# Scan of a hybrid RWKV-7 step: the second stage of an adaLN block moves from the PSUM bank of U to that of Y

## The chip, the cores and the metric

The kernel runs on one core of one Trainium2 chip. The metric is the device time of one execution, in microseconds, as the median over repeated runs. Engines are named as in the profile: PE (matrix products), DVE and ACT (vector and scalar engine), POOL, and SP, whose queue issues most DMAs.

## What is computed

One inference step of a trunk of two layers with D = 1024: a bidirectional RWKV-7 mixer, then neighbourhood attention, each followed by an MLP. There are 128 context tokens and 512 latent tokens. Each sub-layer is modulated by shift, scale and gate from a conditioning vector ("adaLN"); each direction of RWKV-7 runs a delta-rule scan over the tokens:

```python
def ada_mod(cond, w, b):
    m = jax.nn.silu(cond) @ w + b
    return jnp.split(m, 6, axis=-1)
...
def delta_rule_scan(r, w, k, v, kk, a, s0, reverse):
    def step(S, inp):
        r_t, w_t, k_t, v_t, kk_t, a_t = inp
        sa = jnp.einsum('bhvk,bhk->bhv', S, -kk_t)
        S_new = (S * w_t[:, :, None, :] + sa[..., None] * (kk_t * a_t)[:, :, None, :]
                 + v_t[..., None] * k_t[:, :, None, :]).astype(S.dtype)
        y = jnp.einsum('bhvk,bhk->bhv', S_new, r_t)
        return S_new, y
...
    y = (ys[0] + ys[1]).astype(jnp.float32)
    mean = jnp.mean(y, axis=-1, keepdims=True)
    var = jnp.mean(jnp.square(y - mean), axis=-1, keepdims=True)
    yn = ((y - mean) * lax.rsqrt(var + GN_EPS)).reshape(B, T, D) * ln_w + ln_b
    o = (yn + (bonuses[0] + bonuses[1]).reshape(B, T, D)) * g
```

## The kernel before

The scan (`phase_scan`, line 773) works in chunks of 32 tokens. It has five steps n = 0 to 4 of four rounds e = 0 to 3, and in each round one chunk for each direction d = 0 and 1 (`chain_step`, line 1001). A chunk is a chain of four stages. R is the product of the state with the chunk's keys, copied to SBUF (`Rc`, L1035, on ACT). U is the product of Rc with TT, the inverse of a triangular matrix; four GU activations (L1052, ACT) write it into the buffer GU. The state update adds the chunk's products to bank B of its direction, and L1106 (DVE) or L1108 (ACT) copies it into the next GU; where a decay is due, L1111 (DVE) scales the bank. Y is the product of the state with the queries; a copy (L1069, ACT) or, where the other direction has been there already, an addition (L1067, DVE) reads it. R, U and Y of a direction use one PSUM bank A in turn (pool `ch`, one buffer), so each waits for the reader of the one before.

All matmuls of the scan, TensorE's order among them, are pinned by `mm` (line 850) in the order of the code. In a round that is: R d0; what is left of the round before (state update d1 and Y d1, where the fills allow it); U d0; fills; the first stage of an ada block; fills; R d1; state update d0; Y d0; U d1; fills; state update d1. The fills prepare the next step (`prep_group`, line 949): products into a tile `pp`, copies of them on ACT (invA L972, C L974) and a masked product on DVE (L977); POOL, DVE (the scans L916) and ACT (L917, L918, L939) prepare its elements. When a step's fills are done, `invert` (line 979) inverts the triangular matrices on DVE: a mask (L984), a transposition, thirty steps of L993 and L996, and a last transposition to TT (L998), without which the next step's U can't run.

The adaLN sums of layer 0 are made in blocks. `ada_first` (line 279) loads two weight tiles and sums over them on PE, and a copy to SBUF (L289, ACT) follows. `ada_second` (line 292) has two matmuls into four columns of a PSUM tile and one addition on DVE (L300, `mods`). Sixteen blocks of this kind lie in the scan, one first stage in a round; the second stage stands in the next chain step of direction 1 behind its U:

```python
        ut = self.ch.tile([P, 512], F32, name=f"A{d}")
        U = ut[:, :256]
...
        if self.ada_sums and d == 1:
            self.ada_second(*self.ada_sums.pop(0), ut[:, 256:260], self.mm)
        with tc.high_priority():
```

Finished pairs of chunks go through `post_half` (line 1114): loads of V (L1130), the gate (L1131) and factors (L1129) on SP's queue into a buffer `pbuf`; mean (L1136, L1137, L1139), square (L1140, ACT), variance (L1142, L1143) and a root (L258 to L264); V times its factor (L1146) and more (L1147 to L1151); a transposition on PE (L1156); the product with the gate on DVE (L1160); a store on SP's queue (L1162). In step n = 4 the elementwise part runs on DVE, before that on POOL. `wo_first` (line 1182) begins the output projection (L1189 loads, L1191, L1192).

Apart from the pinned order on PE, the order of instructions on each engine comes from a list scheduler with a time model; `tc.high_priority()` puts the operations of the chain ahead of others.

## Time and profile before

| | |
|---|---|
| median of three runs | 2232.8 us (2231.12 to 2234.78) |
| profiled execution | 2239.71 us |
| its span in the trace | 2237.9 us |
| mean granted PE clock | 0.944 |
| PE busy | 2011.6 us (90%) |
| DVE busy | 1169.5 us (52%) |
| ACT busy | 857.0 us (38%) |
| POOL busy | 455.1 us (20%) |
| L1052, GU activations | 160, 60.0 us busy; 64.0 us idle before them for L300 |

The profiled execution took 1.8 us more than its span and 6.9 us more than the median of the runs. The scan lies between some 340 and 780 us of the span; the inversions start (L984) at 440.5, 523.5, 608.6 and 681.8 us in the steps n = 0 to 3. Behind 834 us the MLP, the attention and the second MLP follow, mostly on PE. A row of a timeline merges neighbouring instructions of one kind; in it a matmul of the program counts twice.

### The profile page before, as it was taken

The numbers are of one execution on the slowest core, as the hardware profiler recorded it, in microseconds if no ns is written. First come the engines' busy times: TensorE is split into PE (matmuls) and PEld (weight loads), VectorE is DVE, ScalarE is ACT, GpSimd is POOL, SyncE is SP. The second block draws the span as 40 slices with busy tenths as digits, with TensorE's granted clock in tenths as the row PEclk, the third lists the DMA queues.
The fourth block names the chain that finished last, engine by engine and source line by source line (L and its number), as shares of the span: only waits on it lengthen the run. The fifth ranks groups of instructions, "written<-read, shape, count | busy, mean of one in ns | idle before, by whom it ended". The sixth has DMA issues, their size and how long they took to land.

```text
span 2237.9 us, 44938 instructions
## 1 busy us (share of the span) xinstructions
PE 2011.6 (90%) x18604; PEld 1827.3 (82%) x18604; DVE 1169.5 (52%) x2592; ACT 857.0 (38%) x1712; POOL 455.1 (20%) x553
## 2 busy tenths in 40 slices
PE   6999988757665569999999999999999999999999
PEld 3777777646554568999999998889677999999999
DVE  6656658387679755433333434433666633434342
ACT  4544553546553414313131323221576331313130
POOL 0001275656542411101010110000232110101010
PEclk8997999978787788999999999999899999999999
DMA  6455764545433464323232223343310232222221
GB/s 242 147 157 155 229 205 135 173 133 166 129 132 96 112 187 141 105 76 111 72 111 76 86 76 119 132 135 92 110 57 31 75 122 76 76 76 76 76 74 69
DMA packets 161037, 260.03 MB, mean 116 GB/s; under 512 B 46528, under 2 KB 102976, under 8 KB 160832
## 3 DMA queue, kind: packets, MB, share of 16 engines
q1 hardware_dynamic: 152224, 244.05, 35.2%
q10 hardware_dynamic: 8608, 13.11, 1.7%
q8 instruction: 146, 2.39, 0.4%
q14 instruction: 59, 0.48, 0.1%
HBM read 218.18 MB, written 37.35 MB: 114 GB/s over the span
## 4 chain that ended last, share of the span: by engine, by line
PE 74%; DVE 13%; DMA 5%; POOL 3%; issue 2%; ACT 2%; SPq 1%; DVEq 0%; ACTq 0%; POOLq 0%
PE psl L205 54%; PE psl L239 3%; DVE invX L996 2%; PE ps L1525 2%; DVE invT L993 2%; POOL C L947 2%; PE po L1562 2%; PE pp L852 2%; PE pt L1550 2%; DVE C L977 1%; PE pp L1219 1%; PE psl L1265 1%; PE psl L286 1%; DMA ld_s<-scr 1%; PE A L852 1%
## 5 line engine op out<-in xcount | busy, mean ns | idle before, releaser
L191 ACT CAST whi<-wraw 128x1024 fp32r<-128x1024 f32 x178 | 186.6, 1049 | 731.5 <-PE psl L205 701.9
L205 PE MATMUL psl<-xh,whi 128*128 128x320 f32 (+1 forms) x1696 | 414.6, 317 | 9.6 <-ACT xh L247 4.9
L205 PE MATMUL psl<-xl,whi 128*128 128x320 f32 (+1 forms) x1696 | 410.2, 314 | 1.2 <-DVE xl L248 1.2
L205 PE MATMUL psl<-xh,wlo 128*128 128x320 f32 (+1 forms) x1696 | 409.7, 314 | 0.4 <-DVE ta L592 0.4
L205 PEld LDWEIGHTS psl<-xh,whi 128*128 128x128 f32 x1696 | 291.4, 191 | 28.5 <-issue 8.7
L205 PEld LDWEIGHTS psl<-xl,whi 128*128 128x128 f32 x1696 | 292.5, 191 | 5.7 <-issue 3.2
L205 PEld LDWEIGHTS psl<-xh,wlo 128*128 128x128 f32 x1696 | 292.9, 191 | 2.6 <-issue 1.7
L1172 DVE SCALAR_TENSOR_TENSOR xres<-psl,mods,xres 128x320 f32<-128x320 f32 (+2 forms) x216 | 81.7, 434 | 305.1 <-PE psl L205 305.1
L1345 POOL TENSOR_TENSOR relu<-relu 128x640 f32<-128x640 f32 x64 | 80.2, 1255 | 773.9 <-ACT relu L1344 758.7
L205 PE MATMUL psl<-hhl,whi 128*128 128x320 f32 x1024 | 233.1, 308 | 0.0
L205 PE MATMUL psl<-hhh,wlo 128*128 128x320 f32 x1024 | 233.0, 308 | 0.0
L205 PE MATMUL psl<-hhh,whi 128*128 128x320 f32 x1024 | 232.9, 308 | 0.0
L193 DVE TENSOR_TENSOR wlo<-wraw,whi 128x1024 fp32r<-128x1024 f32 x178 | 218.6, 1229 | 11.6 <-ACT whi L191 10.9
L205 PEld LDWEIGHTS psl<-hhh,whi 128*128 128x128 f32 x1024 | 170.8, 188 | 0.4 <-issue 0.4
L205 PEld LDWEIGHTS psl<-hhh,wlo 128*128 128x128 f32 x1024 | 171.1, 188 | 0.0
L205 PEld LDWEIGHTS psl<-hhl,whi 128*128 128x128 f32 x1024 | 171.0, 188 | 0.0
L1302 DVE TENSOR_TENSOR relu<-psl,rms_b 128x320 f32<-128x320 f32 x128 | 60.8, 486 | 144.6 <-PE psl L205 144.0
L852 PE MATMUL pp<-C,KB 128*64 128x128 f32 x1280 | 100.6, 306 | 39.7 <-DVE C L977 16.7
L852 PEld LDWEIGHTS pp<-C,KB 128*64 128x64 f32 x1280 | 83.0, 154 | 54.1 <-issue 28.8
L248 DVE TENSOR_TENSOR hhl<-relu,hhh 128x640 fp32r<-128x640 f32 x64 | 53.4, 834 | 127.9 <-ACT hhh L247 127.7
L1052 ACT ACTIVATE GU<-A 32x256 f32<-32x256 f32 x160 | 60.0, 375 | 93.2 <-DVE mods L300 64.0
L977 DVE TENSOR_TENSOR C<-pp,cstsb 64x512 f32<-64x512 f32 x80 | 55.0, 688 | 69.1 <-ACT C L974 56.9
(299 smaller groups left out, 3393.2 us busy)
## 6 DMA issues: line engine op xcount, KB each, us to landing
wraw<-in_mlp_w SPq DMA_DIRECT2D x128, 512.0 KB, 3.5
adaraw<-in_ada_w SPq DMA_DIRECT2D x96, 512.0 KB, 4.9
ld_d<-scr SPq DMA_DIRECT2D x20, 512.0 KB, 4.5
ld_s<-scr SPq DMA_DIRECT2D x20, 512.0 KB, 3.7
bias<-in_bias SPq DMA_DIRECT2D x16, 384.0 KB, 3.7
scr<-ta SPq DMA_DIRECT2D x16, 325.0 KB, 3.5
wi<-scr SPq DMA_DIRECT2D x20, 260.0 KB, 4.6
scr<-bp SPq DMA_DIRECT2D x16, 320.0 KB, 4.5
```

What stands on the lines that cost most here:

```text
L191: nc.scalar.copy(hi, raw)
L193: nc.vector.tensor_tensor(lo, raw, hi.bitcast(F32), op=ALU.subtract)
L205: self.nc.tensor.matmul(ps[g][:, :e - c], lhsT=a[:, k, :], rhs=b[:, c:e], start=(k == 0 and j == 0), stop=(k == n - 1 and j == 2))
L239: nc.tensor.matmul(ps, lhsT=a[:, tc_], rhs=w, start=(k == 0 and j == 0), stop=(k == KT - 1 and j == 2))
L248: (lo_eng or nc.vector).tensor_tensor(xl, src, xh.bitcast(F32), op=ALU.subtract)
L852: r = (op or self.nc.tensor.matmul)(*a, **k)
L947: nc.gpsimd.tensor_tensor(rev(o) if s == 0 else o, v4(sh, s, ww)[hs], f[hs], op=ALU.mult)
L977: nc.vector.tensor_tensor(C[o, 8 * h:8 * h + 8, :], pn[o, :, 0:64], mask[o], op=ALU.mult)
L1052: nc.scalar.activation(gu[64 - 64 * hp:96 - 64 * hp, hp, pp].rearrange("p b v -> p (b v)"), U[32 * q:32 * q + 32, :], AF.Copy, scale=-0.5)
L1172: nc.vector.scalar_tensor_tensor(out[:, a:b], ps[g][:, o:o + b - a], gate[:, k, j:j + 1], x[:, a:b], op0=ALU.mult, op1=ALU.add)
L1302: nc.vector.tensor_tensor(t[:, c], ps[q][:, :HALF], rb[:, c], op=ALU.mult)
L1345: nc.gpsimd.tensor_tensor(t, t, t, op=ALU.mult)
```

## The change

`ada_second` leaves the second stage of the chain. Its columns 256 to 259 now lie in the bank of Y, and it stands behind Y's reader and inside `high_priority`, so that its matmuls and its addition have the priority of the chain. Nothing is computed otherwise.

```diff
--- before.py
+++ after.py
@@ -1021,30 +1021,28 @@
         C = [ts["C"][d, hg, ww] for hg in range(2)]
 
         def state_product(s):
-            ps = self.ch.tile([P, 512], F32, name=f"A{d}")[:, :256]
+            pa = self.ch.tile([P, 512], F32, name=f"A{d}")
+            ps = pa[:, :256]
             for ph, pp, hp in idx:
                 q = 2 * hp + pp
                 i = 8 * hp + 4 * ee + 2 * (ph % 2) + pp
                 self.mm(ps[32 * q:32 * q + 32, 64 * ph:64 * ph + 64], lhsT=C[ph // 2][:, i, 32 * s:32 * s + 32],
                         rhs=gu[:, hp, pp, ph, :], start=True, stop=True, tile_position=(0, 32 * q))
-            return ps
-
-        R = state_product(0)
+            return pa, ps
+
+        _, R = state_product(0)
         with tc.high_priority():
             Rc = self.yp.tile([P, 256], F32, name="Rc", bufs=2)
             nc.scalar.copy(Rc, R)
         yield
         TT = ts["TT"]
-        ut = self.ch.tile([P, 512], F32, name=f"A{d}")
-        U = ut[:, :256]
+        U = self.ch.tile([P, 512], F32, name=f"A{d}")[:, :256]
         for ph, pp, hp in idx:
             q = 2 * hp + pp
             o = slice(64 * ph, 64 * ph + 64)
             qs = slice(32 * q, 32 * q + 32)
             self.mm(U[qs, o], lhsT=TT[qs, d * 16 + ((ph // 2) * 4 + cq) * 2 + ph % 2, :],
                     rhs=Rc[qs, o], start=True, stop=True, tile_position=(32 * q, 32 * q))
-        if self.ada_sums and d == 1:
-            self.ada_second(*self.ada_sums.pop(0), ut[:, 256:260], self.mm)
         with tc.high_priority():
             for pp in range(2):
                 for hp in range(2):
@@ -1056,7 +1054,7 @@
             self.state_update(ts, n, e, d, gu, nx, C)
         self.gi[d] += 1
         yield
-        Y = state_product(1)
+        pa, Y = state_product(1)
         tt = ts["tiles"][d]
         with tc.high_priority():
             if tt not in self.yt:
@@ -1068,6 +1066,8 @@
             else:
                 nc.scalar.copy(yo, Y)
                 self.ydone[tt].add(cq)
+            if self.ada_sums and d == 1:
+                self.ada_second(*self.ada_sums.pop(0), pa[:, 256:260], self.mm)
         if e % 2 == 1:
             self.free[ts["par"]] += [ts["C"].pop((d, hg, ww)) for hg in range(2)]
         yield
```

In the changed kernel the lines between are numbered otherwise: Rc is L1036, GU L1050, Y's addition L1065 and its copy L1067.

The orders below show three places. The first is PE at the turn from round e = 0 to e = 1 of step n = 0: A_4169 or A_4166 is R d0, A_4188 or A_4185 is Y d1, A_4206 is U d0, `pp` are fills. Before:

```order
L852 MATMUL A_4169<-GU_3894,C_2648 32x64 [waits DMAHW2_49,PE_49]
L852 MATMUL A_4169<-GU_3894,C_2648 32x64
L852 MATMUL A_4169<-GU_3894,C_2648 32x64 [waits DMAHW3_49]
L852 MATMUL A_4169<-GU_3894,C_2648 32x64 x5
L852 MATMUL A_4169<-GU_3894,C_2656 32x64 x8
L852 MATMUL A_4188<-GU_2638,C_2652 32x64 [waits DVE_49]
L852 MATMUL A_4188<-GU_2638,C_2652 32x64 x7
L852 MATMUL A_4188<-GU_2638,C_2660 32x64 x8
L852 MATMUL A_4206<-Rc,TT 32x64 [waits Activation_49]
L852 MATMUL A_4206<-Rc,TT 32x64 x15
L852 MATMUL pp_4227<-C_3890,KB 64x128 [waits Pool_49] x2
L852 MATMUL pp_4227<-C_3890,KB 64x128 x6
```

And in the change, where the pair (`cstsb,adasb`) stands between Y d1 and U d0 and waits for ACT:

```order
L852 MATMUL A_4166<-GU_3894,C_2648 32x64 [waits DMAHW3_49]
L852 MATMUL A_4166<-GU_3894,C_2648 32x64 x5
L852 MATMUL A_4166<-GU_3894,C_2656 32x64 x8
L852 MATMUL A_4185<-GU_2638,C_2652 32x64 [waits PE_49]
L852 MATMUL A_4185<-GU_2638,C_2652 32x64 x7
L852 MATMUL A_4185<-GU_2638,C_2660 32x64 x8
L852 MATMUL A_4185<-cstsb,adasb 128x2 [waits Activation_49]
L852 MATMUL A_4185<-cstsb,adasb 128x2
L852 MATMUL A_4206<-Rc,TT 32x64 [waits PE_49]
L852 MATMUL A_4206<-Rc,TT 32x64 x15
L852 MATMUL pp_4227<-C_3890,KB 64x128 [waits Pool_49] x2
```

The pair came from behind U d1 of the round before; now U d0 and all fills are behind it and behind its wait.

The second place is DVE at the end of n = 3's inversion, with TT (L998). Before, L1160 runs ahead of TT, and behind it L1106 and Y's addition of direction 1 are followed by L1142, L1136, L1143 and L1192:

```order
L993 TENSOR_TENSOR invT_7843<-invX 128x10
L1160 TENSOR_TENSOR pbuf<-pp_8546,pbuf 128x256 x2
L996 TENSOR_TENSOR invX<-invX,invT_7843 128x10
L998 STREAM_TRANSPOSE TT<-invX 128x32x32
L1106 TENSOR_TENSOR GU_3897<-B_3880,FC 64x512 x2
L1111 TENSOR_TENSOR B_3880<-B_3880,FC 128x512
L1067 TENSOR_TENSOR Y<-Y,A_8421 128x256
L1142 TENSOR_REDUCE yvar<-pbuf 128x8
L1136 TENSOR_REDUCE ysum<-Y 128x8
L1143 TENSOR_SCALAR yvar<-yvar 128x8
L1192 TENSOR_TENSOR ww_9303<-adaraw,ww_9302 128x1024
L1137 TENSOR_SCALAR ysum<-ysum 128x8
```

In the change, L1106, L1111 and Y's addition of direction 0, L1136 to L1139 and L1160 stand behind TT:

```order
L996 TENSOR_TENSOR invX<-invX,invT_7840 128x10
L998 STREAM_TRANSPOSE TT<-invX 128x32x32
L1106 TENSOR_TENSOR GU_3894<-B_3879,FC 64x512 x2
L1111 TENSOR_TENSOR B_3879<-B_3879,FC 128x512
L1065 TENSOR_TENSOR Y<-Y,A_8293 128x256
L1136 TENSOR_REDUCE ysum<-Y 128x8
L1137 TENSOR_SCALAR ysum<-ysum 128x8
L1139 TENSOR_TENSOR Y<-Y,ysum 128x512
```

and these rows follow, in which an L1146 stands ahead of L1136, L1143, L1192 and the addition L300 of the last pair:

```order
L1160 TENSOR_TENSOR pbuf<-pp_8546,pbuf 128x256 x2
L1106 TENSOR_TENSOR GU_3897<-B_3880,FC 64x512 x2
L1111 TENSOR_TENSOR B_3880<-B_3880,FC 128x512
L1065 TENSOR_TENSOR Y<-Y,A_8418 128x256
L1142 TENSOR_REDUCE yvar<-pbuf 128x8
L1146 TENSOR_TENSOR pbuf<-pbuf,bc 128x512
L1136 TENSOR_REDUCE ysum<-Y 128x8
L1143 TENSOR_SCALAR yvar<-yvar 128x8
L1192 TENSOR_TENSOR ww_9303<-adaraw,ww_9302 128x1024
L300 TENSOR_TENSOR mods_96<-A_8418,parsb 128x4
```

Before, the two L1146 came nine and fourteen rows behind that L1142. So operations moved from ahead of TT to behind it, and one that waits for a load moved ahead.

The third place is SP's queue there. pbuf_8343 (in the change pbuf_8340) is stored by L1162, and pbuf_8565 uses the same buffer after it. Before, the loads of two `pbuf` tiles are mixed:

```order
L1162 DMA scr9<-pbuf_8343 128x8x64 [waits DMAHW4_49,DVE_49,Activation_49]
L1130 DMA pbuf_8565<-scr7 32x2x256 [waits DMAHW5_49,DMAHW4_49,Pool_49]
L1130 DMA pbuf_8565<-scr7 32x2x256 [waits DMAHW6_49]
L1130 DMA pbuf_8554<-scr7 32x2x256 [waits DMAHW0_49]
L1130 DMA pbuf_8554<-scr7 32x2x256 [waits DMAHW2_49]
L1130 DMA pbuf_8554<-scr7 32x2x256
L1130 DMA pbuf_8554<-scr7 32x2x256 [waits DMAHW6_49]
L1131 DMA pbuf_8554<-scr10 128x8x64 [waits DMAHW7_49]
L1130 DMA pbuf_8565<-scr7 32x2x256 [waits DMAHW0_49]
L1130 DMA pbuf_8565<-scr7 32x2x256 [waits DMAHW1_49]
L1131 DMA pbuf_8565<-scr10 128x8x64 [waits DMAHW2_49]
```

In the change the four loads of pbuf_8565, the first of which waits for the store, come first:

```order
L1162 DMA scr9<-pbuf_8340 128x8x64 [waits DMAHW4_49,DVE_49,Activation_49]
L1130 DMA pbuf_8565<-scr7 32x2x256 [waits DMAHW5_49,DMAHW4_49,Pool_49]
L1130 DMA pbuf_8565<-scr7 32x2x256 [waits DMAHW6_49]
L1130 DMA pbuf_8565<-scr7 32x2x256 [waits DMAHW7_49]
L1130 DMA pbuf_8565<-scr7 32x2x256 [waits DMAHW0_49]
L1131 DMA pbuf_8565<-scr10 128x8x64 [waits DMAHW1_49]
L1130 DMA pbuf_8554<-scr7 32x2x256 [waits DMAHW3_49]
L1130 DMA pbuf_8554<-scr7 32x2x256 [waits DMAHW5_49]
L1130 DMA pbuf_8554<-scr7 32x2x256 [waits DMAHW7_49]
L1130 DMA pbuf_8554<-scr7 32x2x256 [waits DMAHW1_49]
L1131 DMA pbuf_8554<-scr10 128x8x64 [waits DMAHW2_49]
```

On DVE the first L1146 of the change works on pbuf_8565; before it worked on pbuf_8554.

## Rows read from the trace of the kernel before

**Rows 1.** Chain of waits: engine, line, what it waits for: us, times, longest us

```profile
ACT GU L1052 <- DVE mods L300: 64.0, 15, 13.2
```

**Rows 2.** Busy time by stretches: length, PE (x) PEld DVE ACT POOL, PEclk, DMA share, GB/s

```profile
681.80:725.80 44.00, 22.88 (x560) 18.10 (x560) 43.42 (x152) 14.46 (x33) 11.09 (x9) 0.73 0.31 89
...
834.00:2237.00 1403.00, 1379.79 (x9753) 1305.06 (x9752) 597.83 (x1338) 464.42 (x849) 151.80 (x174) 0.99 0.29 91
```

**Rows 3.** Timeline, PE, n=1: start, us, engine, line, operation [idle before <-releaser]

```profile
504.92 0.61 PE L852 MATMUL A<-cstsb,adasb 128*128 128x2 f32 x4
```

**Rows 4.** Timeline, round n=0 e=1 and the start of n=0's inversion: PE, ACT, DVE

```profile
420.20 0.65 PE L852 MATMUL A<-Rc,TT 32*32 32x64 f32 x32 [0.64 <-ACT Rc L1035]
...
428.49 0.35 ACT L1069 COPY Y<-A 128x256 f32<-128x256 f32 x1
...
434.61 1.97 PE L852 MATMUL pp<-C,KB 128*64 128x128 f32 x32
...
438.87 1.06 ACT L972 COPY invA<-pp 32x128 f32<-32x128 f32 x4
...
439.09 1.39 DVE L1106 TENSOR_TENSOR GU<-B,FC 64x512 f32<-64x512 f32 x2 [2.37 <-PE B L852]
...
440.51 1.22 DVE L984 TENSOR_TENSOR invA<-invA,cstsb 128x1024 f32<-128x1024 f32 x1
```

**Rows 5.** Timeline, DVE, near the end of n=0's inversion

```profile
490.98 1.23 DVE L916 TENSOR_TENSOR_SCAN wi<-cstsb,wi 128x520 f32<-128x520 f32 x1
```

**Rows 6.** Timeline, n=1: ACT, PE, and DVE's start of the inversion

```profile
511.04 0.38 ACT L1069 COPY Y<-A 128x256 f32<-128x256 f32 x1
...
511.19 0.65 PE L852 MATMUL A<-Rc,TT 32*32 32x64 f32 x32 [0.65 <-ACT Rc L1035]
...
519.57 1.75 PE L852 MATMUL pp<-C,KB 128*64 128x128 f32 x28 [0.95 <-issue]
...
523.52 1.23 DVE L984 TENSOR_TENSOR invA<-invA,cstsb 128x1024 f32<-128x1024 f32 x1 [0.82 <-ACT invA L972]
```

**Rows 7.** Timeline, n=2: the last fill on PE, and DVE's start of the inversion

```profile
602.75 1.97 PE L852 MATMUL pp<-C,KB 128*64 128x128 f32 x32 [0.29 <-DVE C L977]
...
608.64 1.22 DVE L984 TENSOR_TENSOR invA<-invA,cstsb 128x1024 f32<-128x1024 f32 x1
```

**Rows 8.** Timeline, n=3: PE and ACT at the start, the last fill, DVE's inversion

```profile
652.88 0.65 PE L852 MATMUL A<-Rc,TT 32*32 32x64 f32 x32
...
653.25 0.35 ACT L1069 COPY Y<-A 128x256 f32<-128x256 f32 x1
...
675.79 1.97 PE L852 MATMUL pp<-C,KB 128*64 128x128 f32 x32
...
681.84 1.23 DVE L984 TENSOR_TENSOR invA<-invA,cstsb 128x1024 f32<-128x1024 f32 x1
```

**Rows 9.** Timeline, DVE, around the end of n=3's inversion (L998) and behind it

```profile
722.94 0.76 DVE L1160 TENSOR_TENSOR pbuf<-pp,pbuf 128x256 f32<-128x256 f32 x2
...
723.81 1.97 DVE L998 STREAM_TRANSPOSE TT<-invX 128x1024 f32<-128x1024 f32 x1
...
728.09 0.68 DVE L1142 TENSOR_REDUCE yvar<-pbuf 128x8 f32<-128x512 f32 x1
...
729.34 1.22 DVE L1192 TENSOR_TENSOR ww<-adaraw,ww 128x1024 fp32r<-128x1024 f32 x1
...
735.04 0.69 DVE L1146 TENSOR_TENSOR pbuf<-pbuf,bc 128x512 f32<-128x512 f32 x1 [0.52 <-issue]
```

**Rows 10.** Timeline, SP's queue; and the chain that ended last, a DMA in it

```profile
726.56 3.69 SPq L1130 DMA_DIRECT2D pbuf<-scr  x6
...
726.92 3.00 DMA pbuf<-scr
```

**Rows 11.** Timeline, PE: R d1 of n=4 e=0 and R d0 of the next round

```profile
728.22 1.08 PE L852 MATMUL A<-GU,C 128*32 128x64 f32 x32 [1.22 <-DVE Y L1067]
...
736.16 1.19 PE L852 MATMUL A<-GU,C 128*32 128x64 f32 x32 [3.10 <-ACT GU L1052]
```

## The prediction

> **What bounds the kernel now.** I read the chain of waits first, then the busy time by stretches, then the timeline step by step. The chain of waits shows the cost that the edit touches: the GU activations (L1052) wait 15 times and 64.0 us in all for the ada addition L300, 13.2 us at the longest [rows 1]. They read columns 0 to 255 of the bank, L300 reads 256 to 259: two readers of one bank run one after the other. The stretches show that little of the 64 us can be got. While a triangular inversion runs, DVE is the bound: 43.42 of 44.00 us busy in the last one; from 834 us to the end PE is busy 1379.79 of 1403.00 us, and nothing of that is touched [rows 2]. So a wait counts only between the end of one inversion (TT, L998) and the start of the next (L984): there the last GU stands on ACT ahead of the invA copies (L972), and L984 needs these.
>
> **What the change does.** It adds and removes no work: 16 pairs of matmuls at 0.6 us [rows 3] and 16 additions move. A pair stood on PE behind U d1 and was waited for by GU alone. It now stands behind Y d1 and waits for Y's reader, and U d0 of the next round, its fills and R d1 queue behind it. GU waits for PE alone. DVE's order shifts too, since the scheduler is run again. I go step by step to TT of n=4, then from there to the end, against the profiled execution (2239.71 us, 6.9 above the median of 2232.8).
>
> **n=0.** U d0 ran at 420.20; the copy of Y d1, late on ACT, ended at 428.49+0.35 = 428.84 [rows 4]. In the change U d0 starts behind it and the pair, at 429.4. R d1, which the same copy released, must now let 4 to 6 us of U and fills pass. Some of this is won back, as R's copy stood behind others on ACT; I put the last fill (434.61+1.97 = 436.58 before) at 440.8, invA's copies 1.06 behind it at 441.9, and L984 right there for 440.51 [rows 4]: +1.4, of which I take +1.3. The ends: if nothing is made up, L984 moves with the fill, +4.2; if the stall cost PE nothing, the fill would end 0.6 earlier (the pair is gone from behind U d1) at 436.0, and L984 could start at 437.0: -3.5. In the inversion behind it, the two L1106 (1.39) that stood ahead of L984 [rows 4] move in: +1.4. A scan L916 (1.23) [rows 5], a reduction L1142 and two small ones (0.8) move out behind TT: -2.05. Together **+0.65**.
>
> **n=1.** Y's copy ends at 511.42, with the pair 512.0; U d0 ran at 511.19: +0.8. The pair is gone from behind U d1: -0.6. The last fill thus ends at 521.32+0.2 = 521.5, GU and L917 no longer hold invA's copies, these end at 522.6, and L984 starts there for 523.52 [rows 6]: **-0.9**.
>
> **n=2.** By the same sum the fill ends at 604.72+0.2 = 604.9, L984 starts at 606.0 for 608.64 [rows 7]: -2.6; there it had stood behind two L1106, which now run behind it: +1.4. Together **-1.2**.
>
> **n=3.** Two pairs stand ahead of a U d0 here. The first costs 653.25+0.35+0.6-652.88 = 1.3 [rows 8]; the second, behind a Y addition on DVE, I put at 0.9, between this and n=1's. Two pairs gone from behind U d1: -1.2. The fill ends at 677.76+1.0 = 678.8, L984 starts at 680.0 for 681.84 [rows 8]: **-1.8**.
>
> **Last inversion.** Two L1106 (1.4), L1160 (0.76), three of the length of L1142 (0.68: L1111, L1136, L1139), a Y addition, L1137 and L300 move from inside to behind TT; an L1142 and small ones move in. By rows 4 and 9 that is some 4.5 out and 0.9 in: **-3.6**. TT of n=4 then ends at 0.65-0.9-1.2-1.8-3.6 = -6.9 against before, at 718.9 for 725.78 [rows 9].
>
> **Behind TT.** This gives the time back. Before, L1160 ran at 722.94, ahead of TT [rows 9]. SP's store L1162 waited for it, and the loads of V behind the store's landing began at 726.56: six issues in 3.69 us, 0.6 apart; the first landed at 726.92+3.00 = 729.92, 3.4 behind its issue [rows 10]. The fourth of four in a row would land at 726.56+1.8+3.4 = 731.8, that is 8.8 us behind the start of L1160. In the change L1160 stands behind TT and L1106, L1111, Y, L1136, L1137 and L1139: by L1106 to the start of L1142 (2.3 us behind TT's end before) and three more at 0.68, 0.17 and 0.68, some 3.9 us behind TT. SP now loads first the buffer that has to wait for the store, and DVE's first L1146 works on just this buffer; it stands ahead of L1136, L1143, two L1192 and L300, where before it stood behind them, at 735.04 with 0.5 us of waiting [rows 9]. So DVE can pass L1146 at 3.9+8.8 = 12.7 us behind TT. Before, it had what now stands behind L1146 still to do at the end of L1142, 728.77, or 3.0 behind TT. What follows is late by 12.7-3.0-0.5 = 9.2 less the 6.9 won: **+2.3 on DVE**. For PE: L1146 at 731.6, then L1136 (0.7), one L1192 (1.22) and a small one, and L300 at some 734.3 [rows 9]; R d1 writes into the bank that L300 reads and runs at 734.4 for 728.22. From there to R d0 of the next round PE needs 736.16-728.22-3.10 = 4.8 [rows 11]: 739.2 for 736.16, **+3.0**. The two meet before 747; I take +2.5, since the chain there runs through DVE, and carry it to the end: 2242.2 for the profiled execution, 6.9 less in the median: **2235.3 us**.
>
> **A rule weighed.** The trace shows two readers of one bank in turn [rows 1]; no row shows a matmul that waits for a reader of other columns. Without such a wait n=0 would be -3.5+1.4-2.05 = -4.2 for +0.65, and the 0.8, 0.8 and 2.2 that the pairs cost in n=1 to n=3 would go: 8.6 less, 2226.7. The order of the change shows the wait on the pair, so I give this no chance of its own. The Trainium skill, PSUM — Partial Sum Buffer, section "PSUM bank collisions raise a hardware error", says that any two engines on one bank and the same quarter of the partitions collide, TensorE's writes against a reader included and in disjoint columns too, and that one has to guard by bank. By that rule Y's bank is no freer than U's: the wait changes its owner, from ACT's GU to PE's queue, and the sum is mine. No run here shows a collision.
>
> **Rivals.** *Faster: the loads are not late.* If V has landed when DVE comes to L1146 (SP free sooner, the store and the landing quicker), nothing is given back and the end moves with TT, -6.9: 2225.9. For it: the 8.8 us rest on one store and one landing, in a stretch where other loads ran beside them. Against: the loads wait for the store by their buffer, and the store for L1160, which now runs behind TT. Decides: idle time of DVE ahead of that L1146 under 3 us. Chance 0.2.
> *Slower: TT gains little.* PE stands behind Y's reader, and the stall of n=0 is not made up. Then L984 of n=0 comes 4.2 late for 1.3, n=3 gives nothing for -1.8, and TT gains 6.9-2.9-1.8 = 2.2 us; with the 9.2 behind TT the end moves by +7.0: 2239.8. For it: in n=0 U d0 ran 8.6 us ahead of the end of Y's copy [rows 4], and n=3's first pair alone stands 1.3 us [rows 8]. Against: L984 waits for ACT, which is freed of GU's wait and L917. Decides: TT of n=4 ends later than 721.5. Chance 0.35.
> *Nothing.* The waits move from GU to U d0 and weigh as much; all else cancels: 2232.8. It lies in my own range, with chance 0.1; my forecast has 0.35.
>
> **How the numbers follow.** About 0.2%, 4.5 us, is what can be told from no change. My forecast (+2.5) and "nothing" lie within it: 0.45. Slower by more: the rival, 0.35. Faster by more: 0.2. The range reaches from the fast rival's time, 2226, to 2242, the slow one's with 2 us more for the store and the landing, which I have from one transfer each; half of the fast rival and the slow one's tail lie outside.
>
> **What would show it.** L1052's wait for L300 is gone from the chain of waits, and PE waits in front of the pair for ACT's L1067 (Y's copy) or DVE's L1065. Against before, L984 of n=0 comes 1 us later, those of n=2 and n=3 some 3 earlier; TT of n=4 ends near 719. Behind it DVE idles about 4 us ahead of L1146, and R d1, at 728.22 before, starts near 734. I am wrong if TT of n=4 ends outside 716 to 722, if DVE does not wait at that L1146, or if the last 1403 us change their length.

## The result and the profile after

The change takes 2251.6 us (median of five runs, 2247.5 to 2253.9) for 2232.9 in the kernel before: ratio 1.0079, with 1.0064 to 1.0094 as its 95% interval. (The ratios here are worked out from the single runs and are not the quotient of the two medians.) It is slower by 18.7 us, and lies 9.6 above the range that was forecast. In a second set of runs it is 2252.0 for 2238.7, ratio 1.0067 (1.0042 to 1.0092). In that and the later sets the kernel before had medians of 2236.2 to 2238.7 over 14 to 30 runs, so that some 3 to 6 us of the 18.7 may be owed to its five runs in the first. One run of a version below, after_first, took 2648.65 us at a granted clock of 0.69 and is in none of its figures. The profiled execution of the change took 2247.51 us, its span 2245.7.

The page of the change: its engines' work and the GU activations, which waited for L300 in [rows 1]. The last line is that of the GU activations on the page of the kernel before:

```profile
PE 2006.0 (89%) x18604; PEld 1823.9 (81%) x18604; DVE 1171.2 (52%) x2592; ACT 858.8 (38%) x1712; POOL 457.1 (20%) x553
...
L1050 ACT ACTIVATE GU<-A 32x256 f32<-32x256 f32 x160 | 60.0, 375 | 64.2 <-PE A L852 55.3
...
L1052 ACT ACTIVATE GU<-A 32x256 f32<-32x256 f32 x160 | 60.0, 375 | 93.2 <-DVE mods L300 64.0
```

The work is the same: as many matmuls, within 6 us of busy time on every engine. The wait for L300 is gone; ACT's idle time in front of GU fell from 93.2 to 64.2 us, most of it now a wait for PE. PE waits for Y's readers instead, in PE's waits over the whole span:

```profile
PE A L852 <- DVE Y L1065: 29.0, 9, 5.6
...
PE A L852 <- ACT Y L1067: 23.4, 10, 10.0
```

All 23.4 us of the second line are waits in front of a pair. Of the first line, 9.2 us in three waits are in front of an R, by PE's timeline; the 16 pairs have 23.4+19.9 = 43.3 us. They replace other waits in part: U's wait for Rc, 14.8 us in 14 times before, is 0.5 in one. The longest is in n=0, in the timeline of PE (start, length, operation, idle time and what ended it), where U d0 ran at 420.20 [rows 4]:

```profile
426.86 1.01 PE L852 MATMUL A<-cstsb,adasb 128*128 128x2 f32 x4 [9.97 <-ACT Y L1067]
427.80 1.07 PE L852 MATMUL A<-Rc,TT 32*32 32x64 f32 x32
```

Behind TT of n=4, DVE (its rows of before are [rows 9]):

```profile
716.31 1.91 DVE L998 STREAM_TRANSPOSE TT<-invX 128x1024 f32<-128x1024 f32 x1
718.08 1.36 DVE L1106 TENSOR_TENSOR GU<-B,FC 64x512 f32<-64x512 f32 x2
...
720.20 0.42 DVE L1065 TENSOR_TENSOR Y<-Y,A 128x256 f32<-128x256 f32 x1
...
722.26 0.75 DVE L1160 TENSOR_TENSOR pbuf<-pp,pbuf 128x256 f32<-128x256 f32 x2
...
726.27 0.68 DVE L1142 TENSOR_REDUCE yvar<-pbuf 128x8 f32<-128x512 f32 x1
730.60 0.69 DVE L1146 TENSOR_TENSOR pbuf<-pbuf,bc 128x512 f32<-128x512 f32 x1 [3.65 <-DMA wr<-in_xT]
...
733.01 0.15 DVE L300 TENSOR_TENSOR mods<-A,parsb 128x4 f32<-128x4 f32 x1
```

The store and loads of SP's queue, for [rows 10], and then PE, for [rows 11]. The store landed 2.6 us behind its issue, at 725.7, right ahead of the loads. The slowest of the four loads landed 3.5 us behind its issue at 727.0, at 730.5 and right ahead of L1146 at 730.60. I take it that L1146 waits for this load, though its row names another transfer:

```profile
723.07 0.38 SPq L1162 DMA_DIRECT2D scr<-pbuf  x1
725.71 1.73 SPq L1130 DMA_DIRECT2D pbuf<-scr  x4
```

```profile
720.67 1.08 PE L852 MATMUL A<-GU,C 128*32 128x64 f32 x32 [5.05 <-DVE Y L1065]
721.68 1.97 PE L852 MATMUL B<-GU,C 64*64 64x64 f32 x32
723.59 0.66 PE L852 MATMUL A<-GU,C 128*32 128x64 f32 x32
726.40 0.61 PE L852 MATMUL A<-cstsb,adasb 128*128 128x2 f32 x4 [2.16 <-DVE Y L1065]
726.94 1.01 PE L852 MATMUL A<-Rc,TT 32*32 32x64 f32 x32
733.22 1.08 PE L852 MATMUL A<-GU,C 128*32 128x64 f32 x32 [5.27 <-DVE mods L300]
...
739.20 0.77 PE L852 MATMUL A<-GU,C 128*32 128x64 f32 x32 [1.35 <-ACT GU L1050]
```

These are R d0, the state update, Y d1, the pair, U d0 (the first with the new TT), R d1 and R d0 of the next round. DVE waits at L1146, L300 runs behind it, R d1 behind L300. In the kernel before, R d0 and U d0 were:

```profile
718.80 1.08 PE L852 MATMUL A<-GU,C 128*32 128x64 f32 x32 [8.46 <-DVE Y L1067]
...
725.92 1.07 PE L852 MATMUL A<-Rc,TT 32*32 32x64 f32 x32 [1.34 <-DVE TT L998]
```

So before, R d0, state update and Y d1 ran ahead of TT (723.81), and U d0 2.1 us behind TT's start. Now they run behind TT, and U d0 is 10.6 us behind its start. The last stretch, from the scan's end to the end (us, then busy time of PE, PEld, DVE, ACT, POOL, and the granted clock), follows. The window of [rows 2] ends 0.9 us ahead of its span's end (2237.9), so that the stretch was 1403.9 us and has grown by 3.1:

```profile
838.70:2245.70 1407.00, 1380.97 (x9752) 1305.46 (x9752) 598.92 (x1338) 464.87 (x849) 151.91 (x174) 0.99 0.28 90
```

Three profiles of each kernel by stretches, in us, from starts read to 0.1 us ("input" is the first transfer of x behind the scan, L1237 in the kernel before, for what is left of the output projection; the expectations call it the attention's input. "Attention" is from the first to the last addition of its scores):

| stretch | before | change | means' difference | forecast |
|---|---|---|---|---|
| start to first TT | 393.1, 395.3, 391.0 | 390.5, 391.1, 390.7 | -2.4 | 0 |
| first to last TT | 330.7, 324.9, 326.1 | 325.8, 327.5, 330.4 | +0.6 | -6.9 |
| last TT to input | 110.2, 112.3, 110.0 | 122.4, 121.3, 123.5 | +11.6 | some +9.4 |
| input to attention | 744.2, 744.7, 744.2 | 744.4, 743.9, 743.7 | -0.4 | 0 |
| attention | 127.2, 126.8, 126.9 | 130.0, 130.0, 129.9 | +3.0 | 0 |
| behind it | 532.5, 532.6, 532.5 | 532.6, 532.4, 532.5 | 0 | 0 |

The sum is +12.4 (spans 2235.1 and 2247.5). Up to the first TT the profiles of both kernels show the same order on DVE, ACT and POOL, and no pair lies there. I take -2.4 as scatter between executions: over the profiles of all kernels on this page the first TT comes at 385.0 to 396.3 us. Two kernels below repeat these scans with only the attention reordered: att_new, the scan of before, has 334.6 us from first to last TT and 110.1 from there to the input; att_old, the scan of the change, 326.0 and 125.2. With them the means' difference is -1.7 from first to last TT and some +12 behind it. So by neither reckoning does the change gain some 7 us ahead of the last TT, and the loss behind it is clear of the scatter. Nor is that loss the granted clock (theory C below): from the last TT to the input it is 0.82, 0.78 and 0.82 in the three profiles of before and 0.79, 0.79 and 0.82 in those of the change, of which the one at 0.82 is the longest.

### The profile page after: what moved, and what is told of

The parts are those of the page before. It is cut to its first block, busy times and chain, and to the rows that moved or that the text cites. A ratio compares the mean times of both kernels' runs of the same rounds, so it can differ in the third digit from the quotient of the medians.

```text
span 2245.7 us, 44954 instructions
## 1 busy us (share of the span) xinstructions
PE 2006.0 (89%) x18604; PEld 1823.9 (81%) x18604; DVE 1171.2 (52%) x2592; ACT 858.8 (38%) x1712; POOL 457.1 (20%) x553
## 4 chain that ended last, share of the span: by engine, by line
PE 74%; DVE 14%; DMA 4%; issue 2%; POOL 2%; ACT 2%; SPq 1%; DVEq 0%; ACTq 0%; POOLq 0%
PE psl L205 53%; PE psl L239 4%; DVE invX L996 3%; DVE invT L993 3%; PE ps L1525 2%; PE pp L852 2%; PE po L1562 2%; POOL C L947 2%; PE pt L1550 2%; DVE C L977 1%; PE pp L1219 1%; PE psl L1265 1%; PE psl L286 1%; PE A L852 1%; PE pk L698 1%
## 5 line engine op out<-in xcount | busy, mean ns | idle before, releaser
L205 PE MATMUL psl<-xh,whi 128*128 128x320 f32 (+1 forms) x1696 | 412.4, 316 | 11.7 <-ACT xh L247 6.2
L1050 ACT ACTIVATE GU<-A 32x256 f32<-32x256 f32 x160 | 60.0, 375 | 64.2 <-PE A L852 55.3
```

What stands on the lines that cost most here:

```text
L205: self.nc.tensor.matmul(ps[g][:, :e - c], lhsT=a[:, k, :], rhs=b[:, c:e], start=(k == 0 and j == 0), stop=(k == n - 1 and j == 2))
L1050: nc.scalar.activation(gu[64 - 64 * hp:96 - 64 * hp, hp, pp].rearrange("p b v -> p (b v)"), U[32 * q:32 * q + 32, :], AF.Copy, scale=-0.5)
```

## Experiments

The theories are those of the expectations: W, orders and waits on DVE behind TT; S, PE's stand in front of the pair; C, the granted clock.

**The change and a pin on L1146**, beside each other. First the unchanged change:

> The changed kernel once more, with every execution's granted clock beside those of the kernel before. Two theories for its 18.7 us. W (waits and orders): DVE waits 3.65 us at an L1146 behind TT of n=4 and the pairs stand on PE; the profiled execution shows about 7 us of this between the first inversion and 834 us, so 7 to 10 us remain for the median, and the other 9 to 12 lie in how the one profiled execution of each kernel stood to its median. C (clock): a part of the loss is a lower granted clock, in which case executions of this kernel fall apart by clock (0.944 at 2247.5, 0.935 to 0.939 at 2249 to 2254 so far) and the kernel before shows a higher clock than the 0.944 of its profiled execution in its faster executions. Expected: 2249 to 2253 again; W: clock of both kernels alike, C: before at 0.947 or more.

2251.95 us, ratio 1.0067 (1.0042 to 1.0092): the loss is there again. The granted clock over an execution is 0.937 to 0.941 for 0.941 to 0.949 in the kernel before; where in the kernel it differs is read below. Then the pin:

```diff
+        vb = el.tensor_tensor(Vg, Vg, bcast(bc.rearrange("p c l -> p (c l)")), op=ALU.mult)
+        if on_dve and tt in (1, 2): self.tc.add_manual_dep(vb.ins, self.root.ins.name, order, reason="order")
```

> The changed kernel with one order on DVE undone: in the two halves that DVE treats in n=4, L1146 (V times its factor) may only run behind the root of its half, as the code has it; it no longer stands ahead of L1136, L1192 and L300. W: DVE's 3.65 us at L1146 go, L300 and R d1 come some 4 us earlier, and with what followed (the lower clock, 3.3 us more to the scan's end) the kernel gains 4 to 7 us: about 2245. S (the stands of PE behind Y's reader are what costs): 0 to 1 us gained, 2251. C: nothing, 2251.

2251.79 us, ratio 1.0063 (1.0040 to 1.0085), runs from 2239 to 2263. The wait at L1146 is gone and the last TT to input takes 117.7 us, in a second profile 119.2, for 121.3 to 125.2: some 3 to 5 us of the 11.6 hang on this wait. The median, which W had at 2245 and S and C at 2251, does not move; half of the runs are at 2255 or above, for a reason that the second profile shows (*More profiles*).

**Another bank for the pair**: the second bank of the fills' tile `pp`, one round later; then with the pin too.

```diff
+                    if self.ada_sums: self.ada_second(*self.ada_sums.pop(0), pa[:, 512:516], self.mm)
```

> The pair in neither bank of the chain: it writes into the second bank of the tile of the next block's first stage, just ahead of that stage's matmuls. GU then never waits for L300 and U never for Y's reader; the order with L1146 early behind TT stays as in the changed kernel. W: the wait at L1146 stays and swallows what is gained, so about 2244 to 2249. S: all stands of PE go (9.97 us in n=0 the longest), the kernel comes to 2233 or below. C: near 2250.

> Both: the pair in neither bank of the chain, and L1146 of the two halves behind the root. W: DVE does not wait behind TT, GU not for L300, PE not for Y's reader; below the kernel before, 2224 to 2231. S: as the kernel with the bank alone, since the order on DVE weighs nothing, about 2233 or below. C: near 2250, as its stretches with little PE work are the same.

2263.39 us (1.0092 to 1.0141) and 2252.59 (1.0044 to 1.0094); W and S had 2224 to 2249 and missed both; C, with near 2250, met the second. PE's waits in the first:

```profile
PE pp L852 <- DVE mods L300: 38.2, 15, 9.4
```

The wait has gone over to the fills; first to last TT grew to 339.5 us, in the second to 341.3.

**The pair in Y's bank, but behind U d0 and the first fills of the next round**, then with the pin:

```diff
-                self.ada_second(*self.ada_sums.pop(0), pa[:, 256:260], self.mm)
+                self.pair.append((*self.ada_sums.pop(0), pa[:, 256:260], self.mm))
```

> The pair keeps Y's bank, but stands on PE behind U d0 and the first fills of the next round instead of ahead of U d0, so that U d0 does not wait for Y's reader (10 us in n=0). L1146 still stands early behind TT. S: the scan gets shorter by what PE loses at Y's reader, to 443 or less, and the kernel is some 5 us faster than the changed one. W: the wait at L1146 stays, and what is won ahead of TT is lost behind it: 446 to 448, no gain over 2 us.

> The pair behind U d0 and the first fills, and L1146 of the two halves behind the root: neither of the two waits is left. W and S: scan of 436 to 441 us, at or below the kernel before (its GU waits for L300 are gone too); the time 0 to 5 us below the kernel before. C: as the changed kernel in the median, 10 us above the kernel before, even if the scan is as short as before.

2258.06 us, ratio 1.0098 (1.0059 to 1.0136), and 2250.10, ratio 1.0045 (1.0022 to 1.0067). Behind TT 115.7 and 114.5 us, some 7 less than in the change, but first to last TT takes 331.5 and 333.7. W and S had the second at or below the kernel before; C had it 10 us above, as it came. In none of these four does the whole come back.

**One order moved.** The gate products L1160 are forced ahead of TT in the change, and behind it in the kernel before. The edit of the change has two orders: `tti` is TT and `og` an L1160; `tgu` is the first L1106 of direction 0, which it holds behind TT, where the change has it:

```diff
+            for a, b in ((self.tti, og), (self.tgu, self.tti)):
+                self.tc.add_manual_dep(a.ins, b.ins.name, mybir.DependencyInfo(
+                    mybir.DependencyClass.NoSync, mybir.DependencyReason.DATA), reason="order")
```

> The change, with one order on DVE put back: the last two L1160 (the gate products of the half that was late) are forced ahead of TT (L998), as in the kernel before, and the L1106 of direction 0 stays behind TT. The pair stays in Y's bank, so PE's stalls in front of it stay. Order theory (W): the whole loss behind TT comes from L1160 standing behind TT, by way of the store, the loads of V behind it and L1146. Then DVE waits under 1 us at the first L1146 behind TT for 3.65, the mods addition of that round is not held, and from the last TT to the first transfer of the attention's input it takes 111 to 113 us as in the kernel before (112.3 and 110.2), for 121.3 to 122.4 in the change; TT itself is 0 to 1.5 us later. The time falls by 8 to 10 us against the change, to some 2243, ratio 1.002 to 1.006. Stall theory (S): PE's stand in front of the pair costs behind TT as well; then 117 us or more stay, as with L1146 pinned (117.8 and 119.2), and the time stays above 2247. Clock theory (C): the loss is the granted clock; then the stretch behind TT shortens by under 3 us in the scan, and the time stays where the change is, 2250 to 2253.

> The kernel before, with one order on DVE changed and nothing else: the last two L1160 (gate products) are tied behind the last transposition to TT (L998), where the change has them. The pair of the ada block stays in U's bank behind U d1. Order theory (W): this alone makes the loss behind TT. TT of n=4 comes 1 to 3 us earlier, since L1160 (2 x 0.76) leaves the inversion; behind it L1162's store and the loads of V are late, DVE waits 2 to 6 us at the first L1146, and from TT to the first transfer of the attention's input it takes 117 to 122 us for 110 to 112. The time is 5 to 9 us above the kernel before, ratio 1.002 to 1.004. Stall theory (S): without a pair in Y's bank PE does not stand, the late L1146 is taken up by DVE's slack, since mods is only waited for by GU; then the stretch stays within 2 us of 111 and the time within 2 us of the kernel before. Clock theory (C): same as S here, no change.

In the change: 2256.61 us (1.0043 to 1.0101), 116.8 us behind TT, DVE still waits 3.15 us at that V product. W said 111 to 113; S, with 117 or more and a time above 2247, is nearer. In the kernel before: 2241.20, ratio 1.0020 (1.0009 to 1.0032), and 112.2 us behind TT; here the V products stayed behind the other work, and DVE waits 0.23 us at the first. W said 117 to 122. That L1160 stands behind TT is not the cause by itself.

**More profiles**: a second and a third of the kernel before, a third of the change (all in the table above), a second of after_pin:

> The kernel before, profiled a second time. Stretches so far: from TT of the step ahead of n=0 (the first L998) to the first transfer of the stage behind the scan (L1237) 440.9 us before, 448.0 and 448.7 in two profiled executions of the changed kernel, and from there to the end 1403.9 against 1407.1 and 1406.3. If the loss lies in the scan (W or S), the first stretch is 440 to 442 again. C: the second stretch depends on the clock alone and lies anywhere from 1402 to 1409; then the 13 to 19 us of the medians hold some 7 us of scan and the rest is the scatter of the executions.

> The changed kernel with L1146 behind the root, profiled a second time, since its executions fell in two groups (2239 to 2248 at a clock of 0.936 to 0.943, and 2256 to 2263 at 0.930 to 0.938). Its scan took 443.3 us where the changed kernel takes 448. W: 443 again, and if the execution is of the longer group the excess lies behind the scan. C: if it is of the longer group, the excess lies where the granted clock is lower, in the scan or in the stages behind it.

> The kernel before, unchanged: a third profile, to see how far one stretch scatters from execution to execution. The first two had 330.7 and 324.9 us from the first TT to the last, and 110.2 and 112.3 us from there to the first transfer of the attention's input. If the forecast's gain ahead of TT was lost by the change itself (stalls of PE, S), this one lies near 331, so that the change's 325.8 and 327.5 are a gain of some 4 us. If the first profile was a long one, it lies near 325 to 327 and the change gains nothing there. Behind TT both theories expect 110 to 113. Clock theory (C): the attention's stretch, 127 us in both, changes with the granted clock in it, by over 2 us for each 0.02 of clock.

> The change, unchanged: a third profile beside a third one of the kernel before on the same chip. From the first TT to the last 325.8 and 327.5 us so far, from there to the first transfer of the attention's input 122.4 and 121.3, the attention 130.0 twice. If the loss is made by the order behind TT (W), this stretch is again 120 to 123, 9 us or more above that of the kernel before. If the attention's 3 us belong to the change, it is again near 130 for 127; if they belong to the granted clock of an execution (C), it moves with the clock of that stretch, in either kernel.

The first profile of before was long ahead of TT, so that the change gains nothing there; behind TT it loses 13.5 in the third pair, and its attention is again 130 us. after_pin scatters most in the attention: 130.6 us in its first profile (2245.79 us) and 140.9 in its second (2260.36), where the granted clock is 0.50 in the second and third 15 us for 0.79 and 1.00. So its upper runs are those with a long attention, as far as one profile can tell.

**The order of the attention.** Its first 111, 85 and 49 instructions on PE, DVE and ACT stand in another order in the change, though the diff does not touch them. Each kernel got the other's:

```diff
+        for e, o in ORDER.items():
+            for a, b in zip(o, o[1:]):
+                self.tc.add_manual_dep(log[e][b].ins, log[e][a].ins.name, mybir.DependencyInfo(
+                    mybir.DependencyClass.NoSync, mybir.DependencyReason.DATA), reason="order")
```

> The change, with the first 111, 85 and 49 instructions of the attention on PE, DVE and ACT forced into the order that they have in the kernel before; all else stands as in the change. Order theory (the new order of the attention costs the 3.0 us): the stretch from the first to the last score addition of the attention takes 126.8 to 127.3 us, as in the kernel before, for 129.9 to 130.0, and the time falls by 2 to 4 us against the change, to some 2249. Clock theory (the granted clock falls at the attention's start by itself, and longer behind the later scan): the stretch stays at 130 us and the time where the change is. The scan stays at 448 to 454 us in both.

> The kernel before, with the first 111, 85 and 49 instructions of the attention on PE, DVE and ACT forced into the order that they have in the change; nothing else is touched, and the ada pair stays in U's bank. Order theory: the attention's stretch takes 129.9 to 130.7 us for 126.8 to 127.2, and the time rises by 2 to 4 us over the kernel before, ratio 1.001 to 1.002. Clock theory: the stretch stays at 127 us and the time within 1 us of the kernel before. The scan stays at 436 to 441 us in both.

The change with the old order: attention 124.4 us; 2250.62 us (1.0032 to 1.0066). The kernel before with the new order: 130.4 us; 2244.36, ratio 1.0024 (1.0005 to 1.0042). Over all eleven profiles with the old order it took 124.2 to 127.3 us. These fall in two: seven of 126.8 to 127.3, with a granted clock of 0.54 in the first 15 us, and four of 124.2 to 124.4, with 0.77. So 2.5 us of att_old's gain are of this other kind, and the order itself is worth some 3. The windows of 15 us from the attention's start, of the kernel before, of the kernel before with the new order, and of the change:

```profile
1578.00:1593.00 15.00, 13.21 (x56) 9.81 (x56) 10.35 (x41) 9.85 (x32) 5.41 (x10) 0.54 0.64 232
1593.00:1608.00 15.00, 15.00 (x103) 10.61 (x102) 10.29 (x38) 10.72 (x32) 3.53 (x6) 1.00 0.13 37
```

```profile
1583.00:1598.00 15.00, 12.60 (x49) 9.06 (x50) 10.83 (x40) 9.78 (x31) 5.06 (x9) 0.53 0.64 229
1598.00:1613.00 15.00, 15.00 (x86) 10.51 (x85) 8.28 (x29) 8.45 (x26) 2.73 (x5) 0.79 0.00 1
```

```profile
1583.00:1598.00 15.00, 11.91 (x51) 8.79 (x52) 10.97 (x41) 9.74 (x32) 5.26 (x10) 0.64 0.65 232
1598.00:1613.00 15.00, 15.00 (x88) 10.44 (x87) 8.10 (x27) 8.51 (x24) 2.90 (x6) 0.79 0.00 1
```

and PE's waits there, of the change:

```profile
PE ps L1525 <- ACT sc L1533: 4.4, 2, 3.8
PE pt L1550 <- ACT ptsb L1552: 1.5, 1, 1.5
```

The first wait is in both kernels. The second, for the copy of a transposed block, stands in the nine profiles with an order of this kind (1.0 to 1.5 us) and in none of the eleven with the old one, and behind it the granted clock (the column behind POOL) is lower: 0.79 in the second 15 us for 1.00. In the change the first 15 us are at 0.64 for 0.54, so that the clock takes (0.54+1.00-0.64-0.79) x 15 = 1.7 us of PE's time and the wait itself 1.5: together the loss of 3.0. In the kernel before with the new order the clock alone makes 3.3 us by the same sum. That the order costs the 3 us is shown; that the wait is what keeps the clock low is read from the profiles, as no run has the wait alone.

**Only the last of the 16 pairs** in Y's bank, or only it in U's; the attention in its old order:

```diff
+        last = self.blocks == 15
+        if self.ada_sums and d == 1:
+            self.blocks += 1
+            if last:
+                self.ada_second(*self.ada_sums.pop(0), ut[:, 256:260], self.mm)
```

(`not last` in the first.)

> The kernel before, with only the last of the 16 pairs moved to Y's bank behind Y's reader; the other 15 stay in U's. The attention is held in its order of before, so that it tells nothing here. On DVE nearly all stands as before, the group of the last round of n=3 and the gate products ahead of TT; the mods addition is now behind TT and the first V product behind it. Stall theory (the pair behind Y's reader makes the loss behind TT): PE waits 2 us in front of the pair and R d1 is late for mods, and from the last TT to the first transfer of the attention's input it takes 115 to 119 us for 110.8. Order theory (the DVE group that was moved behind TT and the first V product make it): 110 to 113 us as before, and the time within 2 us of the kernel before. Half and half would be 114.

> The change, with only the last of the 16 pairs back in U's bank behind U d1; the other 15 stay in Y's. The attention is held in its order of before. On DVE the group of the last round of n=3 (L1111, Y's addition, L1136, L1137, L1139) and the gate products stay behind TT as in the change, and the first V product stays ahead of the next reduction, but the mods addition runs ahead of all these. Stall theory: PE has no pair to stand at and R d1 is not held by mods, so from the last TT to the first transfer of the attention's input it takes 113 to 116 us for the change's 122.4. Order theory: DVE waits 3 to 4 us at the first V product as in the change, and 119 to 123 us stay. The time against the change: 6 to 9 us less by the first, 1 to 3 us by the second, besides 3 us for the attention in both.

y_last: 2239.55 us, ratio 0.9995 (0.9977 to 1.0014), 112.5 us behind TT, as the order theory had it. u_last: 2244.30, ratio 1.0033 (1.0019 to 1.0048), 118.1, between the two theories (113 to 116, and 119 to 123). Against the means of the three profiles the last pair costs 1.7 us where DVE's order is the old one, and 4.3 in the change, where L300 stands behind L1146.

**What the other 7 us are**: u_last with the pin, and u_last with L1160 forced ahead of TT:

> As u_last (15 pairs in Y's bank, the last in U's, the attention in its order of before), and the V product of the tiles 1 and 2 is pinned behind the root of the variance, where it stood in the kernel before, so that DVE comes to it when V has landed. The group of the last round of n=3 stays behind TT. Wait theory: the 3.0 us at the first V product are on the path; from the last TT to the first transfer of the attention's input it takes 113 to 115 us for 118.1, and the time falls by 3 to 5 us against u_last, to some 2240. Group theory: it is the work behind TT (2 x 0.69 of L1106, L1111 0.70, Y 0.42, L1136 0.68, L1137 0.17, L1139 0.69, L1160 2 x 0.37, some 4.8 us) that holds the end; 117 to 119 us stay, and the time is that of u_last within 2 us.

> As u_last, and the gate products of that half, with Y's addition, L1136, L1137 and L1139 that they need, are forced ahead of TT as in the kernel before; the first V product then stands right behind L1106 and L1111. Group theory: from the last TT to the first transfer of the attention's input it takes 111 to 114 us for 118.1, and TT itself comes 2.5 to 3 us later (42 us in the last inversion for 39.3): the time is 2 to 4 us below u_last. Wait theory: DVE waits 2.5 to 4 us at the first V product, the load still under way, 115 to 118 us stay, and the time is that of u_last or up to 2 us above it, since TT is later.

2243.47 us (1.0013 to 1.0043) and 2244.22 (1.0024 to 1.0048); 117.9 and 116.8 us behind TT. Without pair and without wait 117.9 stay, as the group theory had it. But with L1160, Y's addition, L1136, L1137 and L1139 ahead of TT 116.8 stay too, where this theory had 111 to 114 and the wait theory 115 to 118. PE in u_last_pin, where TT's row starts at 718.71:

```profile
723.07 1.08 PE L852 MATMUL A<-GU,C 128*32 128x64 f32 x32 [5.05 <-DVE Y L1071]
725.27 2.37 PE L852 MATMUL B<-GU,C 64*64 64x64 f32 x32 [1.11 <-ACT GU L1056]
727.57 1.08 PE L852 MATMUL A<-GU,C 128*32 128x64 f32 x32
728.58 1.08 PE L852 MATMUL A<-Rc,TT 32*32 32x64 f32 x32
730.38 0.65 PE L852 MATMUL A<-GU,C 128*32 128x64 f32 x32 [0.72 <-DVE Y L1071]
```

R d0 waits for the Y addition of the group that DVE now does behind TT, and the state update, Y d1 and U d0 follow it. In u_last_first, where TT's row starts at 722.93, R d0 waits for L1106 (here L1112), which the edit holds behind TT, and DVE stands at the V product (here L1153) ahead of the L1106 and the Y addition that R d1 needs:

```profile
726.12 1.07 PE L852 MATMUL A<-GU,C 128*32 128x64 f32 x28 [0.25 <-DVE GU L1112]
...
729.18 0.69 DVE L1153 TENSOR_TENSOR pbuf<-pbuf,bc 128x512 f32<-128x512 f32 x1 [2.39 <-DMA pbuf<-scr]
...
732.41 1.08 PE L852 MATMUL A<-GU,C 128*32 128x64 f32 x32 [1.30 <-DVE Y L1071]
```

So u_last_first is no clean test of the group. Where R d1 starts behind TT's start tells the length behind TT in nearly all kernels (us behind TT's start; the kernels are those of this page):

| kernel | U d0 | R d1 | TT to input |
|---|---|---|---|
| before, three profiles, and att_new | 2.1 | 4.4 | 110.0 to 112.3 |
| before_behind | 2.1 | 5.1 | 112.2 |
| y_last | 4.6 | 6.6 | 112.5 |
| pp_bank, pp_pin | 6.9 | 8.8, 8.9 | 115.0, 117.2 |
| y_late_pin | 4.1 | 9.1 | 114.5 |
| u_last_first | 7.1 | 9.5 | 116.8 |
| u_last, u_last_pin | 9.9 | 11.7 | 118.1, 117.9 |
| after_first | 11.2 | 12.2 | 116.8 |
| after_pin, two profiles | 10.6 | 12.6 | 117.7, 119.2 |
| change, three profiles, and att_old | 10.6 to 11.0 | 15.5 to 17.6 | 121.3 to 125.2 |

y_late does not fit it (13.5 and 115.7). The change with the whole group ahead of TT, L1106 of direction 0 too, was not tried, so that this part, 7 us, is read from the profiles and from what the runs exclude; y_last, where the group stands ahead of TT and the last pair in Y's bank, is the nearest, at 112.5. No version beat the kernel before.

## Why the prediction was wrong

The places were right and the sums were not. The forecast was +2.5 us for the profiled execution, the means of the profiles give +12.4. Of the 9.9 between them, 7.5 are the gain ahead of TT that did not come, 3.0 the attention, which was put at nothing, 2.2 the stretch behind TT, and -2.8 the stretches that I take for scatter.

The rival *Slower: TT gains little* is nearest in kind, though the time lies 11.8 above its 2239.8. By its own condition it did not come true: TT of n=4 ended at 718.2, not later than 721.5, and the forecast had 718.9. That this number fits is luck: 2.6 us of it were won ahead of the first TT, where nothing had changed, and the profile that it was set against was the longest of three.

- **Ahead of TT, -6.9: failed, and the largest part of the miss.** By the means of three it is +0.6:

| | forecast | measured |
|---|---|---|
| n=0, first TT to L984 | +1.3 | +2.2 |
| the inversion behind it | -0.65 | +0.8 |
| n=1 | -0.9 | 0.0 |
| the inversion behind it | 0 | +0.1 |
| n=2 | -2.6 | -1.5 |
| the inversion behind it | +1.4 | +1.5 |
| n=3 | -1.8 | +0.1 |
| last inversion | -3.6 | -2.7 |

The steps that failed are the gains in n=1 to n=3, 5.3 us forecast and 1.4 measured. Only the last two inversions in the table are clear of what the executions of one kernel differ by (40.5 to 40.9 us before and 42.1 to 42.2 in the change; 42.0 and 39.3); n=3 alone took 29.8 to 33.2 us with the scan of before. I read it so that PE's stand in front of the pairs, 43.3 us in all, took what the pair behind U d1 no longer costs; no run has the scan without both, so that this part stays open. What the steps of before cost came from one profile, 5 to 6 us longer from first to last TT than its two repeats.

- **Behind TT, +9.4 with the 6.9 won: the size nearly right, the cause half.** R d1 was put at 734.4 and ran at 733.22; R d0 of the next round came at 739.20, as forecast; L1146 at 730.60 for 731.6. (The landing at 729.92 that went into this is that of a load issued at 726.92, 3.0 us before; the load issued at 726.56 landed 2.5 us behind its issue. This is worth under 1 us.) The stretch lost 11.6. But I took the whole loss to be the wait at L1146. That wait with the pair is worth 4 to 5: both are absent from u_last_pin, and 7 stay. The step that failed here is *Last inversion*: I booked the group that leaves it (-3.6) as DVE time alone. Its L1106 and its Y addition are what R d0 waits for (the one its input, the other the bank's reader), and behind R d0 PE has a state update, Y d1 and the pair to do before U d0. A TT that comes 2.7 us earlier is of no use if the chain gets to it 8.5 later. This is argued from the profiles, as said above.
- **"Carry it to the end": failed.** The last 1403.9 us grew by 3.1, which I had named as a sign of being wrong: 3.0 by the order of the attention, of which I had written that nothing is touched.
- **The rule weighed** (the Trainium skill, PSUM — Partial Sum Buffer, section "PSUM bank collisions raise a hardware error": guard by bank and quarter of the partitions, or simply by bank, and not by address) agrees with the waits of this program, and no run shows a collision: GU no longer waits for L300, and the pair, in other columns than Y, waits for Y's reader, 43.3 us in 16 times. In a third bank (pp_bank) the wait went to the fills, 38.2 us in 15 times.
- **The priority half** of the edit is not shown by itself: no run has Y's bank at the same place without `high_priority`, or U's bank with it.

In all: +0.6 - 2.4 - 0.4 ahead of and around the scan's stages, +11.6 behind TT, +3.0 in the attention, +12.4 between the means of the profiles; the medians differ by 13.2 in the second set of runs and by 18.7 in the first, and what is left of the 18.7 stays open. Of theory C this remains: the granted clock goes with part of the loss in the attention, and the stretches on both sides of it have the same length in both kernels, within 0.4 us.

## What to carry to other kernels

A wait for a shared PSUM bank does not go away with another bank that has readers too; ask which queue it joins, and what stands behind it there. When instructions leave a busy stretch of one engine, follow what each of them releases on the others before the gain is booked. Where a list scheduler orders the whole program, compare the order to the very end: an edit here changed the order of a stage that starts some 800 us later.

## What was not expected

- A wait of 1.0 to 1.5 us of PE, 9 us into the attention, goes with a longer stay at the lower of the two clock levels: in the second 15 us the granted clock is 0.78 to 0.81 in eight profiles with such a wait and 0.50 in a ninth, and 1.00 in all eleven without it. The stage took 129.8 to 130.6 us in the eight and 140.9 in the ninth, 124.2 to 127.3 without the wait.
- Executions of one kernel differ by more than the stage at issue: first to last TT took 324.9 to 330.7 us in the kernel before and 325.8 to 330.4 in the change, with the same instruction order on DVE, ACT and POOL in each, and 334.6 in att_new, whose scan is that of before.
